# Seven products instead of eight in the attention's output projection, and a fixed order of transposes and products on TensorE

## The chip, the cores and the metric

The kernel runs on one core of one Trainium2 chip. A core has TensorE (PE in the profile; PEld are its weight loads), VectorE (DVE), ScalarE (ACT), GpSimd (POOL) and SyncE (SP), which here only issues DMAs. The metric is device time in microseconds (us) for one execution; lower is better.

## The reference

One layer of an encoder for two sequences of 1024 rows and 1024 columns. Attention and a Fourier mixing run side by side on the same normalised input and share one output projection; a feed-forward part (FFN) follows. What matters here is the attention and its half of the projection:

```python
def attend(args):
    qn_b, qp_b = args
    sc = (jnp.einsum('bqhd,bkhd->bhqk', qn_b, k_nope)
          + jnp.einsum('bqhr,bkr->bhqk', qp_b, k_pe)).astype(jnp.float32) * scale
    p = jax.nn.softmax(sc, axis=-1).astype(v.dtype)
    return jnp.einsum('bhqk,bkhd->bqhd', p, v)
...
mix = jnp.concatenate([y_mla, y_four], axis=-1) @ w_out
x = x + ga1 * mix
h2 = rmsnorm(x, g_ffn) * (1.0 + sc2) + sh2
ffn = (jax.nn.silu(h2 @ w_gate) * (h2 @ w_up)) @ w_down
return x + ga2 * ffn
```

The attention has 4 heads of width 128, so its half of the projection multiplies 512 columns by a 512 x 1024 part of `w_out`. Everything is float32. The kernel writes a product of two float32 matrices as three matmuls (`mm3`, lines 78 to 81): each operand is split into a high part (a cast on ScalarE, line 63) and a low part (the difference, line 64, on VectorE unless told otherwise), and high x high, high x low and low x high are added up.

## The kernel before

**Stages.** Up to about 282 us of the profile: adaLN, input projection and Fourier mixing. Then the attention of both sequences, to about 714 us; then the FFN, by products of half matrices, to the end. The attention is what the change touches, with its turn into the FFN.

**The attention** is a loop of 64 items k, one for each sequence s, block b of 256 rows, head h and half block u of 128 rows. Eight items make a block; r is k mod 8. Step k does, in the program's order:

- `scores(k)`: ten matmuls of 512 columns into `ps_s`; VectorE takes the maximum (`mx`, `nb`), ScalarE the exponential into `p`, VectorE scales by the reciprocal of the sum.
- in r = 3 and 4 `rope_q` (six matmuls of 256 columns and the rotary arithmetic, with `hv`, for the next block), in r = 5 and 6 `rope_flip` (four transposes into `pqt`, read out into `qp`), and in odd steps `absorb_q` (six matmuls of 256 columns, split into `qa`).
- `values` in r = 5 and 1: 24 matmuls of 512 columns for two heads and 256 rows, split into the high and low parts `o0b` and `o1b`.
- `flip_p(k-1)`: eight transposes of the probabilities of the item before, in two groups (`ppt`), each split into `pt`.
- ten steps behind its first score, the projection of a block: `out_proj` in r = 2, 4, 6 and 0, one for each u and each half g of the 1024 columns. Each is 12 matmuls (four heads, three each) into a bank `gb`, added on VectorE to the row tile `x`, which already holds the residual and the Fourier part. `norm2` normalises a finished row tile (ScalarE's square, six small GpSimd operations, VectorE's scaling into `xn`) in r = 4 and 0, `flip_h` transposes it (eight transposes, `pht`) in r = 6 and, for the other half, in r = 2.

The weights of the projection are made twice, for each sequence: loaded (`wv_load`), multiplied on GpSimd by the gate row `gah` (`wv_gate`, in steps 5 and 9 and in 37 and 41; the row's second half is loaded between) and split into `wv` (`wv_split`, eight splits in steps 6 to 11 and 39 to 43).

**The order.** The program is written with tiles; a scheduler puts each engine's instructions in a fixed order ahead of time, by the program's order and by when it expects the operands. `tc.issue_after(i)` holds the instructions under it behind instruction i, `first(early, late)` puts one before another, and `behind()` means behind the last split. Where neither stands, the scheduler may put transposes in the middle of a product. A tile with `bufs=n` has n buffers, and a writer waits for the reader of the oldest. `gb` and the transposes' banks have two each.

**The turn into the FFN.** Blocks (0,0) to (1,1) are projected in the loop. Block (1,2) is projected in steps 64 to 67, around the last `flip_p` and the last `values`; its row tiles are loaded in steps 60 and 61. Block (1,3) follows in four products behind the loop. Between them stand the FFN's preparations: `prep_h` splits the transposed rows into `H` (halves of 128 x 1024), `sums_w` makes four sums of the first FFN weights, `flip2` transposes the rows of block (1,2) and `norm3` normalises those of (1,3). `tail.close()` gives the memory back.

## Time and profile before

| | us |
|---|---|
| median of three runs | 1994.22 (1994.19 to 1996.29) |
| the profiled execution | 1991.72 |
| its span, first to last instruction | 1989.9 |
| attention, from the profile's timeline | about 282 to 714 |
| granted TensorE clock, mean | 0.998 |

The profile is one execution. In a timeline a row gives start, duration, engine, line, operation, output <- inputs, shapes and how many were merged; in brackets stands the idle time before it and what ended it. Matmuls are pipelined, and the durations shown overlap: what a matmul costs TensorE is the distance between two starts. A group row gives busy time and mean duration in ns, then the engine's idle time just before.

### The profile page before, as it was taken

How to read it: one execution, taken by the hardware profiler on the slowest of the kernel's cores; microseconds unless marked ns; L12 is line 12 of the kernel's file. 1: busy time of each engine (PE TensorE's matmuls, PEld its weight loads, DVE VectorE, ACT ScalarE, POOL GpSimd, SP SyncE). 2: the span in 40 equal slices, each digit the busy share in tenths (PEclk: the TensorE clock that was granted, in tenths of full speed). 3: DMA queues.
4: the chain of work that ended last, by engine and by line, in shares of the span. 5: the costliest groups of instructions: out<-in, count | busy, mean ns of one | idle time of the engine just before them, and what ended most of it. 6: DMA issues, size and time to landing. Idle time of an engine off the chain costs nothing.

```text
span 1989.9 us, 27639 instructions
## 1 busy us (share of the span) xinstructions
PE 1965.3 (99%) x9554; PEld 1621.7 (81%) x9554; DVE 1382.5 (69%) x2081; ACT 893.7 (45%) x1743; POOL 831.0 (42%) x1008
## 2 busy tenths in 40 slices
PE   8999999999999999999999999999999999999998
PEld 6788778888888878888888888888888888888886
DVE  5667767666777687877767668779655665656794
ACT  5764545555565563333333355443333333335551
POOL 2554012111312348977877401345644544510152
PEclk9999999999999999999999999999999999999999
DMA  9986965535354584654655597774322322357762
GB/s 392 333 318 227 358 237 116 110 91 160 101 117 138 191 283 166 218 181 172 200 182 190 171 316 231 239 230 150 133 96 90 132 94 92 116 199 241 254 228 85
DMA packets 167081, 377.12 MB, mean 190 GB/s; under 512 B 18044, under 2 KB 43260, under 8 KB 163740
## 3 DMA queue, kind: packets, MB, share of 16 engines
q1 hardware_dynamic: 144252, 304.03, 45.2%
q0 software_dynamic: 22112, 70.27, 11.4%
...
## 4 chain that ended last, share of the span: by engine, by line
PE 59%; DVE 2%; issue 1%; POOL 1%; DMA 1%; ACT 0%; SPq 0%; POOLq 0%; DVEq 0%; ACTq 0%
PE bank L80 20%; PE bank L79 20%; PE bank L81 20%; DVE wl L64 1%; DMA draw<-in_w_down_dram 1%; DVE val L1987 0%; DVE val L154 0%; DVE val L1878 0%; DVE H L64 0%; DMA val<-x_d 0%; POOL rs_y L107 0%; POOL val L154 0%; DVE val L151 0%; POOL out_dram L1993 0%; DVE val L1875 0%
## 5 line engine op out<-in xcount | busy, mean ns | idle before, releaser
L79 PE MATMUL bank<-H,wh 128*128 128x512 f32 x1232 | 480.2, 390 | 2.6 <-DVE val L154 0.9
L80 PE MATMUL bank<-H,wh 128*128 128x512 f32 x1232 | 479.5, 389 | 0.3 <-DVE H L64 0.3
L81 PE MATMUL bank<-H,wl 128*128 128x512 f32 x1232 | 479.3, 389 | 0.2 <-DVE wl L64 0.2
L79 PEld LDWEIGHTS bank<-H,wh 128*128 128x128 f32 x1232 | 231.2, 188 | 53.2 <-DVE val L1861 2.0
L64 DVE TENSOR_TENSOR wl<-draw,wh 128x512 fp32r<-128x512 f32 x286 | 209.0, 768 | 94.0 <-ACT wh L63 93.5
L81 PEld LDWEIGHTS bank<-H,wl 128*128 128x128 f32 x1232 | 231.3, 188 | 49.0 <-DVE wl L64 0.5
L80 PEld LDWEIGHTS bank<-H,wh 128*128 128x128 f32 x1232 | 231.3, 188 | 48.2 <-DVE H L64 0.6
L154 DVE TENSOR_TENSOR val<-bank,val 128x512 f32<-128x512 f32 x200 | 136.6, 689 | 163.0 <-PE bank L81 162.1
L63 ACT CAST wh<-draw 128x512 fp32r<-128x512 f32 x286 | 164.9, 619 | 173.2 <-PE bank L80 131.6
L154 POOL TENSOR_TENSOR val<-val 128x512 f32<-128x512 f32 x58 | 82.4, 1421 | 345.7 <-DVE val L1959 163.5
L80 PE MATMUL bank<-wl,wh 128*128 128x512 f32 x572 | 223.2, 390 | 0.8 <-DVE wl L64 0.5
L63 ACT CAST wh<-rgu 128x512 fp32r<-128x512 f32 x172 | 107.1, 623 | 258.4 <-PE bank L80 203.2
L81 PE MATMUL bank<-wh,wl 128*128 128x512 f32 x572 | 222.6, 389 | 0.0
L79 PE MATMUL bank<-wh 128*128 128x512 f32 x572 | 222.6, 389 | 0.0
L63 ACT CAST wh<-val 128x512 fp32r<-128x512 f32 x133 | 82.3, 622 | 261.9 <-PE bank L80 249.3
L64 DVE TENSOR_TENSOR wl<-val,wh 128x512 fp32r<-128x512 f32 x133 | 126.1, 950 | 65.4 <-ACT wh L63 65.3
L64 DVE TENSOR_TENSOR wl<-rgu,wh 128x512 fp32r<-128x512 f32 x172 | 162.5, 945 | 0.8 <-ACT wh L63 0.7
L151 POOL TENSOR_TENSOR val<-rgu 128x512 f32<-128x512 f32 x80 | 108.3, 1354 | 78.7 <-DMA rgu<-in_wgu_dram 74.9
L80 PEld LDWEIGHTS bank<-wl,wh 128*128 128x128 f32 x572 | 107.4, 188 | 25.2 <-DVE wl L64 2.9
L79 PEld LDWEIGHTS bank<-wh 128*128 128x128 f32 x572 | 107.4, 188 | 22.5
L81 PEld LDWEIGHTS bank<-wh,wl 128*128 128x128 f32 x572 | 107.4, 188 | 21.9
L151 POOL TENSOR_TENSOR val<-val 128x512 f32<-128x512 f32 x89 | 119.1, 1356 | 1.3
...
## 6 DMA issues: line engine op xcount, KB each, us to landing
...
```

The source lines that it names most:

```text
L63: here["a"] = nc.scalar.copy(hi, src).ins
L64: here["v"] = (eng or nc.vector).tensor_tensor(out=lo, in0=src, in1=rd(hi), op=ALU.subtract).ins
L79: nc.tensor.matmul(out, lh, rh, start=first, stop=False, skip_group_check=cont)
L80: nc.tensor.matmul(out, lh, rl, start=False, stop=False, skip_group_check=cont)
L81: here["t"] = here["pe"] = nc.tensor.matmul(out, ll, rh, start=False, stop=last, skip_group_check=cont).ins
L151: return eng.tensor_tensor(out=out, in0=x, in1=y, op=ALU.subtract).ins
L154: eng.tensor_tensor(out=out, in0=x, in1=y, op=ALU.add)
```

## The change

The projection of a block is a product of two matrices that are each cut in 2 x 2: the rows of the block by u and the heads by pairs (a11, a12, a21, a22), the weights by pairs of heads and by g (b11, b12, b21, b22). Winograd's form of Strassen's method needs seven products of such parts instead of eight, with sums around them:

- weights: b12 - b11, b22 - b12, b22 - (b12 - b11) and b21 - that, made in place by `wv_sum` on GpSimd; seven parts are split, fourteen splits a sequence;
- rows: `left_half` (at the first `values` of a block) makes a11's split and s3 = a11 - a21; `right_half` (at the second) splits a12 and a22 and makes s2, a21 + a22 and s4; the low parts of the sums are made on GpSimd (`low`);
- products m1 to m7, six matmuls each, one a step in r = 2 to 7 and 0, in the order of `PROD`; m1 is copied to `u`, m6 is added to it, and that goes to three quarters of the rows on GpSimd; the others are added on VectorE to one or two quarters each.

Every product is held behind the step's `flip_p`, and `flip_h` behind the product. `norm2` and `flip_h` take u = 1 first. `rope_flip` goes from r = 6 to 7. `p`, `qp`, `qa` and `hv` lose one buffer each, `H60` and `H61` are allocated when the tail is closed, and the rows of (1,3) are normalised in place. Block (1,2) has four of its products in steps 58 to 61 and three behind `flip_p(62)`; its row tiles are loaded in step 57.

```diff
     def half(name):
-        return e.tile([P, 512], F32, tag="hv", name=name, bufs=2)
+        return e.tile([P, 512], F32, tag="hv", name=name, bufs=1)
...
-        qp = e.tile([P, HEADS, P], F32R, tag="qp", name="qp", bufs=4)
+        qp = e.tile([P, HEADS, P], F32R, tag="qp", name="qp", bufs=3)
...
-        qa = [e.tile([P, 256], F32R, tag=f"qa{i}", name=f"qa{i}", bufs=3) for i in range(2)]
+        qa = [e.tile([P, 256], F32R, tag=f"qa{i}", name=f"qa{i}", bufs=2) for i in range(2)]
...
+    PROD = ("m1", "m7", "m6", "m5", "m4", "m2", "m3")
+    WEIGHT = {"m1": 0, "m2": 1, "m3": 2, "m5": 3, "m6": 4, "m7": 5, "m4": 6}
...
+    def low(t, src, eng):
+        here["a"] = nc.scalar.copy(t[0], src).ins
+        eng.tensor_tensor(out=t[1], in0=src, in1=rd(t[0]), op=ALU.subtract)
+
+    def left_half(s, b, po):
+        f = S["f", s, b] = {"a21": rest("fa"), "s3": rest("fs")}
+        o = S["o", s, b] = {"m1": part("oa")}
+        nc.scalar.copy(f["a21"], po[:, :, 1, :])
+        split(*o["m1"], po[:, :, 0, :])
+        sub(f["s3"], po[:, :, 0, :], f["a21"], nc.vector)
+
+    def right_half(s, b, po):
+        f, o = S["f", s, b], S["o", s, b]
+        for k, u in (("m2", 0), ("m4", 1)):
+            o[k] = part(("ob", "oc")[u])
+            split(*o[k], po[:, :, u, :])
+        s2, s4 = rest("ft"), rest("fu")
+        sub(s2, po[:, :, 1, :], f["s3"], nc.vector)
+        add(f["a21"], f["a21"], po[:, :, 1, :], nc.vector)
+        sub(s4, po[:, :, 0, :], s2, nc.vector)
+        for k, v in (("m6", s2), ("m5", f["a21"]), ("m3", s4)):
+            o[k] = part(f"o{k}")
+            low(o[k], v, nc.gpsimd)
...
-        for h in range(HEADS):
-            mm3(pm, o[0][:, h, us], o[1][:, h, us], wv[0][:, h, gs], wv[1][:, h, gs], h == 0, h == HEADS - 1)
-        here["v"] = nc.vector.tensor_tensor(out=x2[:, gs], in0=x2[:, gs], in1=pm, op=ALU.add).ins
+        for c in range(2):
+            with tc.issue_after(here["tp"]):
+                mm3(pm, lh[:, c, :], ll[:, c, :], wv[0][:, wi, c, :], wv[1][:, wi, c, :], c == 0, c == 1)
+        if k == "m1":
+            S["u"] = tl.tile([P, 512], F32, tag="u", name="u", bufs=1)
+            nc.scalar.copy(S["u"], pm)
+            o["m7"] = part("oa")
+            low(o["m7"], S.pop(("f", s, b))["s3"], nc.gpsimd)
...
+        for u, g in {"m1": ((0, 0),), "m7": ((1, 0), (1, 1)), "m5": ((1, 1), (0, 1)), "m4": ((1, 0),), "m2": ((0, 0),),
+                     "m3": ((0, 1),)}.get(k, ()):
+            to(u, g, pm)
+        if k == "m6":
+            here["v"] = nc.vector.tensor_tensor(out=S["u"], in0=S["u"], in1=pm, op=ALU.add).ins
+            for u, g in ((1, 0), (1, 1), (0, 1)):
+                to(u, g, S["u"], nc.gpsimd)
...
-                nc.tensor.transpose(pt[:, c, :], xn[:, (4 * g + c) * P : (4 * g + c + 1) * P], ident)
+                with tc.issue_after(here["t"]):
+                    nc.tensor.transpose(pt[:, c, :], xn[:, (4 * g + c) * P : (4 * g + c + 1) * P], ident)
...
-        if i % 2 == 0:
-            out_proj(s, b, i // 4, i // 2 % 2)
-        if i in (2, 6):
-            norm2(s, b, i // 4, tl)
-        if i == 4:
-            flip_h(s, b, 0)
+        if i < 7:
+            out_proj(s, b, i)
+        if i in (4, 6):
+            norm2(s, b, 3 - i // 2, tl)
+        if i == 6:
+            flip_h(s, b, 1)
...
-            p = w.tile([P, N], F32, tag="p", name="p", bufs=3)
+            p = w.tile([P, N], F32, tag="p", name="p", bufs=2)
...
+        def wv_sum(out, x, y):
+            for c in range(2):
+                o, x_, y_ = (S["wv", 2 * (blk // 2) + c, blk % 2] for blk in (out, x, y))
+                with tc.issue_after(here["p"]):
+                    here["p"] = sub(o, x_, y_, nc.gpsimd)
...
+        for q, k0 in enumerate((4, 36)):
+            for i in range(8):
+                todo[k0 + i // 4].append(lambda i=i: wv_gate(i))
+                if i == 3:
+                    todo[k0].append(lambda q=q: gate_half(q, 1))
+            for d, k, blk, sums in ((2, "m1", 0, ((0, 1, 0), (1, 3, 1))), (4, "m7", 1, ()), (4, "m3", 3, ((3, 3, 0),)),
+                                    (5, "m6", 3, ()), (6, "m5", 0, ()), (6, "m2", 2, ((2, 2, 3),)), (7, "m4", 2, ())):
...
-            todo[60 + u].append(lambda u=u: out_load(1, 2, u))
+            todo[57].append(lambda u=u: out_load(1, 2, u))
...
+                if k == nit:
+                    out_proj(1, 2, 4)
+                    norm2(1, 2, 1, tl)
+                    for i in (5, 6):
+                        out_proj(1, 2, i)
+                    S["tail", 3] = here["v"]
...
-                    if i in (5, 6):
-                        rope_flip(*nxt[:2], i - 5, tbank)
+                    if i in (5, 7):
+                        rope_flip(*nxt[:2], i // 2 - 2, tbank)
...
+            if 48 <= m < 52:
+                out_proj(1, 2, m - 48)
...
-        for n in range(4):
-            out_proj(1, 3, n // 2, n % 2)
-            if n == 1:
-                norm3(0)()
-            prep_step((2, 0, 0, 0)[n])
-            if n == 1:
+        for n in range(7):
+            out_proj(1, 3, n)
+            if n == 4:
+                norm3(1)()
+            prep_step((0, 2, 0, 0, 0, 0, 0)[n])
+            if n == 4:
```

81 lines of the change are left out of this document (36 added, 45 removed).

## The prediction

> **What bounds the kernel now.** I read the page's busy table first, then the busy time by stretches, then TensorE's own timeline, because its busy figure counts pipelined matmuls twice.
>
> ```profile
> PE 1965.3 (99%) x9554; PEld 1621.7 (81%) x9554; DVE 1382.5 (69%) x2081; ACT 893.7 (45%) x1743; POOL 831.0 (42%) x1008
> ```
> ```profile
> 440.00:494.60 54.60, 54.46 (x301) 46.10 (x300) 36.01 (x69) 30.13 (x63) 8.41 (x20) 1.00 0.57 141
> 714.00:722.00 8.00, 6.85 (x29) 4.76 (x27) 7.86 (x13) 7.25 (x12) 1.63 (x2) 1.00 0.87 297
> 722.00:730.00 8.00, 7.67 (x35) 6.25 (x36) 8.00 (x8) 7.59 (x9) 6.52 (x8) 1.00 0.56 204
> 730.00:738.00 8.00, 7.34 (x39) 5.86 (x38) 7.93 (x12) 4.34 (x9) 1.86 (x2) 1.00 0.79 277
> 738.00:746.00 8.00, 8.00 (x37) 6.62 (x36) 7.97 (x9) 5.34 (x11) 5.09 (x4) 1.00 0.66 215
> 746.00:754.00 8.00, 8.00 (x37) 6.53 (x36) 5.57 (x7) 2.37 (x4) 7.59 (x8) 1.00 0.53 188
> ```
>
> The columns of the stretches are length, then busy time of PE, PEld, DVE, ACT and POOL, the granted clock, the DMA share and GB/s. The first is one block of the attention (eight steps): TensorE is full, VectorE has 36.0 us of 54.6. The others are the start of the FFN: there VectorE is full from 714 to 746 (31.8 of 32 us) and TensorE has gaps. So a matmul saved inside the attention is time saved; one saved just ahead of 714 is not, unless VectorE also gets there earlier.
>
> ```profile
> 403.32 0.40 PE L79 MATMUL gb<-pt,ckv 128*128 128x512 f32 x1
> ...
> 408.54 0.39 PE L81 MATMUL gb<-pt,ckv 128*128 128x512 f32 x1
> 408.77 1.03 PE L1424 MATMUL ppt<-ident,p 128*128 128x128 f32 x8
> 409.56 0.48 PE L1395 MATMUL ps_s<-lat,qa 128*128 128x512 f32 x1
> 409.88 0.40 PE L1396 MATMUL ps_s<-lat,qa 128*128 128x512 f32 x1
> ...
> 412.22 0.63 PE L1424 MATMUL ppt<-ident,p 128*128 128x128 f32 x4
> 412.60 0.47 PE L79 MATMUL gb<-wv,o0b 128*128 128x512 f32 x1
> 413.06 0.66 PE L1424 MATMUL ppt<-ident,p 128*128 128x128 f32 x4
> 413.47 0.48 PE L80 MATMUL gb<-wv,o0b 128*128 128x512 f32 x1
> 413.79 0.40 PE L81 MATMUL gb<-wv,o1b 128*128 128x512 f32 x1
> ```
>
> From the 1st to the 24th matmul of one `values` the starts move by 5.22 us: **0.227 us a matmul of 512 columns**, though each is shown as 0.39. Eight transposes in a row take 0.79 us, and the matmul behind them 0.32, which is 0.09 more. Split by one matmul (412.22 to 413.79) the same eight and two matmuls take 1.57 us, against 0.79 + 0.32 + 0.23 = 1.34 together.
>
> **The change, part by part.**
>
> *Products.* Before, a block takes 4 products of 12 matmuls, after 7 of 6: 42 for 48. Over eight blocks 48 fewer, 48 x 0.227 = **-10.9 us**, if TensorE is the limit wherever they go.
>
> ```profile
> 423.36 0.39 PE L80 MATMUL gb<-wv,o0b 128*128 128x512 f32 x1
> 423.88 0.96 PE L1424 MATMUL ppt<-ident,p 128*128 128x128 f32 x7
> ```
>
> *Order.* Counted in the timeline, a block has 13 runs of transposes; after the change 12. At most 0.23 (the split above), 0.09 (a run) and 0.29 are won, the last in step r = 0, where two matmuls of a product go ahead of `flip_p` and the transposes start 0.52 us after the second instead of 0.23. Against that, nothing fills in for late probabilities. Bounds over six blocks 0 and -3.6; I take **-2.0**.
>
> *Work of the other engines in a block.*
>
> ```profile
> L1404 DVE TENSOR_REDUCE mx<-ps_s 128x1 f32<-128x1024 f32 x9 | 11.0, 1222 | 7.8 <-PE ps_s L1399 7.8
> L64 DVE TENSOR_TENSOR pt<-ppt,pt 128x512 fp32r<-128x512 f32 x16 | 10.5, 682 | 0.4 <-ACT pt L63 0.3
> L1411 DVE TENSOR_SCALAR p<-p,rr 128x1024 f32<-128x1024 f32 x8 | 6.1, 760 | 0.2
> L1343 DVE TENSOR_TENSOR x<-x,gb 128x512 f32<-128x512 f32 x4 | 2.7, 678 | 0.5 <-PE gb L81 0.5
> L64 DVE TENSOR_TENSOR qa<-gb,qa 128x256 fp32r<-128x256 f32 x4 | 1.7, 416 | 0.0
> L64 DVE TENSOR_TENSOR o1b<-gb,o0b 128x512 fp32r<-128x512 f32 x2 | 1.4, 693 | 5.7 <-ACT o0b L63 5.7
> L1409 ACT ACTIVATE p<-ps_s,nb 128x1024 f32<-128x1024 f32 x8 | 9.0, 1120 | 1.8 <-DVE nb L1405 1.7
> L63 ACT CAST qa<-gb 128x256 fp32r<-128x256 f32 x4 | 1.5, 372 | 4.2 <-PE gb L81 4.2
> L1468 POOL TENSOR_TENSOR wvr<-wvr,gah x16: 1277/1290/1748, 295.4 to 545.4; 128x512 f32<-128x512 f32 x16
> ```
>
> VectorE loses 4 adds and 2 splits (4 x 0.678 + 2 x 0.693 = 4.1 us) and gets 9 adds of 512 columns and 7 operations of 256 (3 low parts, 3 differences, 1 sum; the form of `qa`): 9 x 0.678 + 7 x 0.416 = 9.0. Net +4.9: 40.9 us in a block of about 52.9. ScalarE gets eight casts of 0.372 and one copy twice as wide for two casts twice as wide, +2.2. GpSimd gets 3 adds of 1.29 and 4 differences half as wide: +6.5 on 8.4. None becomes the bound on average. In step r = 3 it is close: 3.7 us of softmax and `pt`, 1.4 of the rotary query, 0.4 of `qa`, 1.4 for the two adds of m7 make 6.8 us, times 0.9 because neighbours overlap (the forms of that block sum to 40.2 where 36.0 are busy) 6.1 us, beside TensorE's ten scores, twelve half-wide matmuls, eight transposes and six matmuls, 5.9 us. What queues there drains in r = 5, where `values` alone gives 5.4 us. Between the last score of a step and the transposes of its probabilities stand at least eight transposes, six matmuls and the next ten scores, with the half-wide ones 5.2 us.
>
> *Weights.* Fourteen splits a sequence for eight, and eight GpSimd differences, in steps 4 to 11 and 36 to 43. The second four gatings follow the first in the next step, not four later, behind the load of the gate's other half, which itself waits for the first four. GpSimd stands there, with the norm chains of steps 38 and 40 behind it; the transposes of those rows come two steps later, which covers it. In steps 38 to 43 TensorE has some 36 us; VectorE has 0.77 x 36 = 27.9 and 14 x 0.68 = 9.5, or 37.4: 1.3 us too much there. Bounds: 0 if hidden, 12 x 0.68 = 8.2 if all the new ones are in the open; near the lower end, **+1.5**.
>
> *The last block's turn.* Four products of block (1,2) go up to steps 58 to 61 and three stay, behind `flip_p(62)`.
>
> ```profile
> 682.00 0.39 PE L1399 MATMUL ps_s<-lat,qp 128*128 128x512 f32 x1
> 683.62 0.74 DVE L1411 TENSOR_SCALAR p<-p,rr 128x1024 f32<-128x1024 f32 x1
> 694.94 0.39 PE L81 MATMUL gb<-pt,ckv 128*128 128x512 f32 x1
> 707.10 0.98 PE L1647 MATMUL pht<-ident,xn 128*128 128x128 f32 x7 [0.78 <-DVE xn L1353]
> 714.55 0.39 PE L79 MATMUL bank<-H,wh 128*128 128x512 f32 x1
> ```
> ```profile
> L64 DVE TENSOR_TENSOR H<-H,H 128x1024 fp32r<-128x1024 f32 x6 | 7.1, 1219 | 0.0
> ```
>
> The last score starts at 682.00, so TensorE is free at 682.23. The probabilities of item 62 are scaled at 684.36; before, a product stood in that gap. After, the products there must follow the transposes: 684.36 - 682.23 = 2.1 us, or 0.9 if VectorE scales before it takes the maximum of item 63 (1.2 us, in between). I take the upper end, **+2.1**, since that order is not touched.
>
> Then `values` ends: its last matmul starts at 694.94, the FFN's first at 714.55, 19.4 us after that matmul's 0.23. In them lie 72 matmuls of products; after the change 36 (one product of (1,3), m1, can stand before `values`). So 8.2 of the 10.9 us are to be had here. VectorE, though, has from there on: 5 operations of the right half (2.1), the 4 sums of the first FFN weights (2.7), 9 adds (6.1), 4 halves of `H` (4.9), two norms like the scaling of `p` (1.5): 17.3 us, times 0.9 some 15.6, and starts 0.3 after `values`. Its adds also give back the two `gb` banks, so TensorE waits with it. The FFN then starts about 16.0 us after `values`: 3.4 earlier instead of 8.2, **+4.8** lost. Bounds: +1 if VectorE is no limit (one wait like that of 0.78 us at 707.10 remains), +8.2 if the start doesn't move at all, since VectorE is full from 714 on.
>
> *At nothing.* `p` with 2 buffers: the exponential of item k needs the transposes of k-2, which TensorE ends a step before; uncovered it costs one exponential, 1.1 us, a step. `qp` 3, `qa` 2, `hv` 1: the last reader of the buffer is a step or a head earlier; uncovered, a cast of 0.4. `rope_flip` in step 7 has `absorb_q` behind it, so the transposes' banks come back in time. The row loads of (1,2) go from steps 60 and 61 to 57 in SP's queue, ahead of later `comb_h` loads; their buffers come free with the norms of (1,1) in 54 and 56. `H60` and `H61` behind the tail's end: split only after the FFN's first weights. `norm3` in place waits on its own store, which the norm's chain covers; if not, VectorE's adds queue behind it, within the turn's bound of 8.2.
>
> *Sum.* -10.9 - 2.0 + 1.5 + 2.1 + 4.8 = **-4.5 us**. The profiled execution took 1991.72 us (span 1989.9 and 1.8 around it), so 1987.2. It lies 2.5 us under the median of the runs; against the median 1994.22 that is **1989.7 us**.
>
> **The rivals.**
>
> A. *VectorE is no limit at the turn:* TensorE's order there can be filled and the 36 matmuls are saved whole. For it: in the attention VectorE idles a third. Against: 31.8 of 32 us behind it. -10.9 - 3 + 0.5 + 1 + 1 = -11.4, or 1982.8.
>
> B. *The FFN doesn't start earlier:* VectorE's extra adds eat the turn. For it: the full stretches. -10.9 - 1 + 1.5 + 2.1 + 8.2 = -0.1, or 1994.1.
>
> C. *Softmax becomes the limit of the steps (slower).* The place is the 5.2 us between a step's scores and its transposes. The chain there has maximum 1.22, exponential 1.12, scaling 0.76 and small ones, some 4.0 with the time between them (an estimate: 3.1 in the rows), plus whatever stands ahead on VectorE. It decides from 1.2 us of queue on, that is when two adds stand ahead in r = 3, 4, 6. GpSimd also slows VectorE:
>
> ```profile
> 641.48 0.75 DVE L1411 TENSOR_SCALAR p<-p,rr 128x1024 f32<-128x1024 f32 x1
> 651.67 1.58 DVE L1411 TENSOR_SCALAR p<-p,rr 128x1024 f32<-128x1024 f32 x1
> ```
> ```profile
> 650.97 1.74 POOL L151 TENSOR_TENSOR hcb<-hca 128x512 f32<-128x512 f32 x1
> ```
>
> The same scaling takes 0.75 us alone and 1.58 while GpSimd subtracts, and GpSimd gets 6.5 us more a block. With 0.6 us in three steps of six blocks, 10.8 us, the sum is +6.3, or 2000.5. [...]
>
> D. *TensorE's clock falls in the gap at the turn.* If the wait of the turn, 4.8 us, lies in one piece and the granted clock halves for as long afterwards, 4.8 us give half the matmuls: +2.4, so -2.1 in all, or 1992.1.
>
> ```profile
> 0.00:10.00 10.00, 4.76 (x20) 4.50 (x21) 3.52 (x14) 1.50 (x2) 1.69 (x9) 1.00 0.84 309
> ```
>
> Here TensorE idles 5.2 us of 10 and the clock is given as 1.00, which speaks against it. [...]
>
> That the change doesn't do what it says: the product count is fixed by the program, but the order already is nearly the new one (13 runs for 12); that is the 0 in the order's bounds.
>
> **How the numbers follow.** Forecast 0.45 (its own range -1.5 to -8), A 0.25, B 0.14, C 0.12, D 0.04. A measurement of this kernel can tell about 0.2%, 4 us, from no change. Faster by more: A and 0.27 of the forecast's 0.45 (its middle is only just past 4 us), 0.52. Within: the other 0.18, B and D, 0.36. Slower: C, 0.12. The range from 1983 to 1997 leaves out the far half of A and most of C; it takes in the weights' bound of 8.2 us.
>
> **What would show it.** Right: a block of 52.9 us in the attention; 336 matmuls that read `wv` instead of 384; a wait of some 2 us on `p` behind item 63's scores; VectorE full from the end of `values`, the FFN's first matmul some 16 us behind it, with TensorE waiting on adds (`gb`) or on `wl`. Wrong: a block above 53.5 with waits on `nb` or `p` in steps 3, 4 and 6 (C); FFN's start 12 us or less behind `values` (A) or still 19 (B); waits in steps 38 to 43 on `wv` above 2 us.

## The result, and the profile after

The changed kernel takes 2024.03 us (median of four runs, 2022.76 to 2025.32); the kernel before, on the same chip, 1994.2 us (1991.45 to 1996.29). The ratio is 1.015, 95% interval 1.0133 to 1.0168: **slower by some 30 us**, where 1989.7 was forecast and 1997 was the end of the range. The profiled execution after took 2022.76 us, with a span of 2020.6.

The page of the changed kernel, its busy table and the line of the granted clock (40 slices of the span, tenths):

```profile
PE 1966.4 (97%) x9506; PEld 1617.6 (80%) x9506; DVE 1435.0 (71%) x2173; ACT 917.3 (45%) x1811; POOL 911.6 (45%) x1080
PEclk9999999999999989999999999999999999999999
```

TensorE has 48 matmuls fewer (9506 for 9554), as it should, and a busy time that is no shorter. The span is 30.7 us longer, so TensorE now has time in which it has nothing to do, or works slowly: one slice has a granted clock of only 8 tenths.

Where the time went is read from TensorE's own timeline. `values` starts sixteen times, at marked places of the attention, and the FFN's first matmul reads `wh`. These rows of the changed kernel (start, duration, engine, line, operation) are the starts of `values` groups 1, 3, 9, 12, 15 and 16, the last matmul of group 16, and the FFN's first:

```profile
301.16 0.40 PE L79 MATMUL gb<-pt,ckv 128*128 128x512 f32 x1
...
355.45 0.48 PE L79 MATMUL gb<-pt,ckv 128*128 128x512 f32 x1
...
515.20 0.48 PE L79 MATMUL gb<-pt,ckv 128*128 128x512 f32 x1
...
607.01 0.40 PE L79 MATMUL gb<-pt,ckv 128*128 128x512 f32 x1
...
686.01 0.40 PE L79 MATMUL gb<-pt,ckv 128*128 128x512 f32 x1
...
707.28 0.48 PE L79 MATMUL gb<-pt,ckv 128*128 128x512 f32 x1
...
713.02 0.39 PE L81 MATMUL gb<-pt,ckv 128*128 128x512 f32 x1
...
742.45 0.50 PE L79 MATMUL bank<-H,wh 128*128 128x512 f32 x1 [0.71 <-ACT wh L63]
```

The same starts in both kernels give this table. The last columns are the product matmuls counted in the stretch (those that read `wv`), what their difference is worth at 0.227 us each, and what is left over.

| stretch (groups) | before, us | after, us | difference | products before, after | worth | left |
|---|---|---|---|---|---|---|
| to group 1 | 300.7 | 301.2 | +0.5 | 0, 0 | 0 | +0.5 |
| first preparation of weights (1 to 3) | 48.0 | 54.3 | +6.3 | 24, 18 | -1.4 | **+7.7** |
| three undisturbed blocks (3 to 9) | 163.9 | 159.8 | -4.1 | 144, 126 | -4.1 | 0.0 |
| second preparation (9 to 12) | 81.4 | 91.8 | +10.4 | 72, 66 | -1.4 | **+11.8** |
| late steps (12 to 15) | 76.5 | 79.0 | +2.5 | 48, 60 | +2.7 | -0.2 |
| last scores (15 to 16) | 19.2 | 21.3 | +2.1 | 24, 24 | 0 | +2.1 |
| turn (16 to the FFN) | 24.85 | 35.2 | +10.3 | 72, 42 | -6.8 | **+17.1** |
| the rest | 1275.4 | 1278.1 | +2.7 | | | +2.7 |

The last row is no effect of the change in itself: over all kernels below that keep the FFN's order, the rest lies between 1275.4 and 1279. In the experiments "turn" is from group 15 to the FFN: 44.1 us before, 56.4 after.

**The saving is there where nothing disturbs it.** A window of one block in the changed kernel (columns as in the prediction: length; PE, PEld, DVE, ACT, POOL; granted clock; DMA share; GB/s):

```profile
408.80:462.06 53.26, 53.26 (x295) 44.79 (x294) 40.17 (x79) 31.99 (x70) 14.45 (x28) 1.00 0.43 100
```

TensorE is full and VectorE has 40.2 us, close to the 40.9 that were worked out.

**What is lost lies in two places.** The waits of TensorE in the changed kernel (who waited for what: us in total, times, longest), the largest ones of the attention and the turn:

```profile
PE gb L79 <- DVE xn L1386: 6.8, 2, 5.8
...
PE ppt L1476 <- DVE nb L1457: 4.6, 4, 2.1
PE ppt L1476 <- DVE p L1463: 3.1, 3, 2.1
PE gb L79 <- DVE fu L151: 2.9, 1, 2.9
PE ps_s L1449 <- DVE qa L64: 2.8, 2, 2.0
...
PE gb L79 <- DVE qt L1022: 2.1, 1, 2.1
...
PE pht L1705 <- DVE xn L1404: 2.0, 1, 2.0
```

`p`, `qa` and `qt` belong to the preparations; the longest wait on `nb` is that of the last scores, the 2.1 us forecast there (VectorE makes `nb` of item 63 right behind the scaling of p(62), and the wait is put down to it); `xn` at line 1386, `fu` and `xn` at line 1404 are the turn. All that are shown are waits for VectorE. In the stretches of the two preparations TensorE's waits come to 6.4 and 7.6 us (1.5 of these for ScalarE), where the kernel before has 0.6 and none.

*Preparation.* A stretch of the second one in the changed kernel, first VectorE's and GpSimd's timelines, then TensorE's (in brackets: idle before, and what ended it):

```profile
527.61 3.01 POOL L1517 TENSOR_TENSOR wvr<-wvr,gah 128x512 f32<-128x512 f32 x2 [3.47 <-DMA gah<-ga_d]
...
529.46 1.71 DVE L64 TENSOR_TENSOR wv<-wvr,wv 128x512 fp32r<-128x512 f32 x1
531.09 1.75 DVE L1463 TENSOR_SCALAR p<-p,rr 128x1024 f32<-128x1024 f32 x1
...
536.05 1.75 DVE L1404 TENSOR_SCALAR xn<-x,rs_r 128x1024 f32<-128x1024 f32 x1 [2.08 <-POOL rs_r L111]
```
```profile
532.98 1.39 PE L1476 MATMUL ppt<-ident,p 128*128 128x128 f32 x8 [2.05 <-DVE p L1463]
...
534.60 0.63 PE L80 MATMUL gb<-wv,ob 128*128 128x512 f32 x1
535.02 0.63 PE L81 MATMUL gb<-wv,ob 128*128 128x512 f32 x1
```

GpSimd waits 3.5 us for its load and then multiplies just while VectorE splits weights. The split takes 1.71 instead of 0.68, the scaling of `p` behind it 1.75 instead of 0.75, and the transposes wait 2.05 us. VectorE itself then stands for 2.08 us before the norm's scaling, whose reciprocal root comes from GpSimd behind the gatings. Behind TensorE's wait the eight transposes take 1.39 us (1.03 elsewhere) and matmuls start 0.42 apart, not 0.23: TensorE runs at half speed for a while (granted clock 0.58 in 532.98:536.73).

*Turn.* The whole stretch before, then after, and four microseconds of it:

```profile
689.70:714.55 24.85, 24.03 (x113) 19.43 (x112) 16.31 (x21) 13.51 (x22) 7.78 (x21) 1.00 0.76 274
```
```profile
707.30:742.50 35.20, 22.30 (x86) 16.42 (x83) 20.95 (x30) 15.95 (x28) 14.80 (x26) 0.85 0.61 218
...
724.00:728.00 4.00, 4.00 (x10) 3.09 (x10) 2.12 (x4) 3.26 (x5) 2.42 (x5) 0.50 0.85 333
```

Before, TensorE was busy in 24.0 of 24.9 us there. After, no engine is: VectorE has 21 of 35 us, GpSimd nearly twice what it had. That looks like a chain of waits, not like a full engine. TensorE's four longest waits there, and the GpSimd row behind the last of them:

```profile
716.27 0.47 PE L79 MATMUL gb<-wv,oa 128*128 128x512 f32 x1 [2.87 <-DVE fu L151]
...
723.65 0.77 PE L79 MATMUL gb<-wv,oa 128*128 128x512 f32 x1 [5.77 <-DVE xn L1386]
...
730.71 0.87 PE L1705 MATMUL pht<-ident,xn 128*128 128x128 f32 x6 [1.99 <-DVE xn L1404]
...
738.72 0.50 PE L79 MATMUL gb<-wv,ob 128*128 128x512 f32 x1 [1.06 <-DVE xn L1386]
```
```profile
734.20 3.75 POOL L1386 TENSOR_TENSOR xn<-xn,u 128x512 f32<-128x512 f32 x3 [4.33 <-DVE u L1392]
```

Read in order: m1 of (1,3) waits until `fu`, the last operation of the right half, has read the bank of `values`; m7 waits for m1's add, which stands on VectorE behind two halves of `H` and three of the four sums; the transposes wait for the norm behind (1,2)'s last add, itself held behind the fourth sum; m2 waits for an add that VectorE makes only when GpSimd has done m6's three adds. The releasers show this sequence; which link is worth what, only the runs can show. The waits of 6.8, 2.9, 2.0 and 0.7 us on TensorE and one of 0.4 make 12.8, where before there was one of 0.8; 14 matmuls of the stretch start 0.43 apart, 2.9 us more; together 14.9 of the 17.1 left over.

### The profile page after: what moved, and what is told of

Its sections match the earlier page's. It is cut to its first block, busy times and chain, and to the rows that moved or that the text cites. A ratio compares the mean times of both kernels' runs of the same rounds, so it can differ in the third digit from the quotient of the medians.

```text
span 2020.6 us, 27899 instructions
## 1 busy us (share of the span) xinstructions
PE 1966.4 (97%) x9506; PEld 1617.6 (80%) x9506; DVE 1435.0 (71%) x2173; ACT 917.3 (45%) x1811; POOL 911.6 (45%) x1080
## 3 DMA queue, kind: packets, MB, share of 16 engines
q10 hardware_dynamic: 576, 1.05, 0.1%
## 4 chain that ended last, share of the span: by engine, by line
PE 84%; DVE 6%; DMA 3%; POOL 3%; ACT 2%; issue 2%; SPq 0%; POOLq 0%; ACTq 0%; DVEq 0%
PE bank L79 22%; PE bank L80 22%; PE bank L81 22%; PE gb L79 2%; PE gb L80 2%; PE gb L81 2%; PE ppt L1476 2%; PE ps_s L1449 1%; PE ps_s L1450 1%; PE ps_s L1451 1%; PE ps_s L1447 1%; PE ps_s L1448 1%; DVE mx L1456 1%; DVE wv L64 1%; DVE p L1463 1%
```

## The experiments

All results in one table: time of the kernel (the median with the 95% interval of its ratio to the kernel before, or a single run) and the stretches, read as above.

| kernel | time, us | ratio to before | first prep. | 3 blocks | second prep. | late | turn | rest |
|---|---|---|---|---|---|---|---|---|
| before | 1994.2 | 1 | 48.0 | 163.9 | 81.4 | 76.5 | 44.1 | 1275.4 |
| after | 2024.03 | 1.0133 to 1.0168 | 54.3 | 159.8 | 91.8 | 79.0 | 56.4 | 1278.1 |
| b_order | 1997.9 | single run | 47.9 | 163.9 | 81.4 | 76.5 | 46.2 | 1278.9 |
| a_free | 2019.0 | single run | 54.3 | 158.9 | 88.7 | 77.8 | 57.4 | 1277.7 |
| a_nosum | 2014.6 | single run | 51.2 | 159.7 | 87.2 | 79.0 | 56.6 | 1278.1 |
| a_sumdve | 2027.6 | single run | 57.5 | 159.7 | 93.1 | 78.9 | 57.6 | 1277.9 |
| a_spread | 2020.2 | single run | 51.5 | 161.8 | 89.4 | 79.0 | 56.4 | 1278.5 |
| a_eight | 2020.7 | 1.0114 to 1.0145 | 50.0 | 160.3 | 90.3 | 79.0 | 57.9 | 1277.3 |
| a_none | 2011.0 | 1.0067 to 1.0097 | 48.1 | 160.3 | 85.0 | 79.0 | 56.4 | 1278.3 |
| n_gate | 2009.7 | 1.0056 to 1.0086 | 48.1 | 160.2 | 82.4 | 79.0 | 58.0 | 1277.2 |
| a_turn | 2025.2 | single run | 54.3 | 159.5 | 91.6 | 79.0 | 54.4 | 1283.2 |
| a_banks | 2023.0 | single run | 54.3 | 159.7 | 91.5 | 79.0 | 57.9 | 1276.8 |
| a_both | 2020.6 | single run | 51.5 | 161.8 | 90.3 | 78.9 | 56.3 | 1278.1 |
| a_cover | 2027.7 | 1.0147 to 1.0178 | 54.6 | 159.7 | 92.8 | 78.9 | 61.3 | 1276.8 |
| a_norm | 2023.4 | 1.0128 to 1.0162 | 54.4 | 159.7 | 92.9 | 79.0 | 56.2 | 1276.3 |
| a_early | 2027.0 | 1.014 to 1.0174 | 54.3 | 159.6 | 91.6 | 79.0 | 54.9 | 1284.5 |
| a_fill | 2026.0 | 1.0138 to 1.0169 | 54.3 | 159.6 | 91.5 | 79.0 | 58.9 | 1277.4 |
| a_first | 2022.1 | 1.012 to 1.015 | 54.3 | 159.7 | 91.8 | 79.0 | 54.1 | 1277.2 |
| a_fb | 2021.4 | 1.0123 to 1.0157 | 54.3 | 159.7 | 92.7 | 79.0 | 53.8 | 1276.9 |
| a_best | 2030.4 | 1.0156 to 1.0187 | 56.6 | 161.8 | 90.3 | 79.2 | 55.6 | 1285.5 |

Each stretch is from one profiled execution. How far it repeats is seen in kernels whose edit does not touch it: the late steps are 78.9 to 79.2 wherever the products' order stands, the first preparation 54.3 to 54.6, the second 91.5 to 92.9, the turn 56.4 to 58.0. So 1 us can be read in the first two of these, but only some 2 us in the second preparation and at the turn. The turn column holds the last scores too, and in some kernels these take 22.9 us instead of 21.3, since the clock is halved there (see the last section). Where that matters, the time from group 16 to the FFN is given: 35.2 us in the changed kernel, 34.8 to 36.7 in the seven kernels in which the turn is as the change made it.

### The order of transposes and products

**b_order**: the kernel before, with the order alone.

```diff
-            mm3(pm, o[0][:, h, us], o[1][:, h, us], wv[0][:, h, gs], wv[1][:, h, gs], h == 0, h == HEADS - 1)
+            with tc.issue_after(here["tp"]):
+                mm3(pm, o[0][:, h, us], o[1][:, h, us], wv[0][:, h, gs], wv[1][:, h, gs], h == 0, h == HEADS - 1)
...
-                nc.tensor.transpose(pt[:, c, :], xn[:, (4 * g + c) * P : (4 * g + c + 1) * P], ident)
+                with tc.issue_after(here["t"]):
+                    nc.tensor.transpose(pt[:, c, :], xn[:, (4 * g + c) * P : (4 * g + c + 1) * P], ident)
```

> The kernel before, with only the new order: each product held behind the step's flip_p, flip_h behind the product; eight products as before. Theory 1 (the order is nearly the old one and harmless): within 3 us of the kernel before, a steady block of the attention 54.0 to 54.8 us for 54.6. Rival (the order is what costs, since no product fills in for late probabilities): 10 us or more slower, a block of 56 or more.

The blocks take 163.9 us with it and without; only the last scores change, where the turn column grows from 44.1 to 46.2. So the order is worth nothing in the blocks, and costs the 2.1 us at p(62). The time is 2.9 us above the 1995.0 of the kernel before, run beside it: theory 1.

**a_free**: the changed kernel without the order (the same two holds taken out).

```diff
-            with tc.issue_after(here["tp"]):
+            with ExitStack():
                 mm3(pm, lh[:, c, :], ll[:, c, :], wv[0][:, wi, c, :], wv[1][:, wi, c, :], c == 0, c == 1)
...
-                with tc.issue_after(here["t"]):
+                with ExitStack():
```

> The changed kernel without the fixed order: products and flip_h free again. Theory 1 (the cost lies in the weights' preparation and in the turn to the FFN, not in the order): still 2012 us or more, 0 to 10 us less than the changed kernel, the turn (from the last values to the FFN's first matmul) still above 30 us for 35.2. Rival (the order costs): 1998 or less.

The blocks gain 0.9 us, the late steps 1.2 and the second preparation 3.1: where probabilities are late, a product may now go ahead of their transposes. The first preparation and the turn are as long as with the order, as theory 1 had it. So the order makes the second preparation's loss larger and is not the cause of it.

### The preparation of the weights

**a_nosum**: the changed kernel without the differences and sums of the weights on GpSimd, which are left out.

```diff
-                for out, x, y in sums:
+                for out, x, y in ():
```

> The changed kernel without the weights' sums (wv_sum left out: 8 GpSimd differences a sequence less; all splits stay, so the sums of the projection are not the reference's). Theory 1 (GpSimd's work beside VectorE's makes VectorE's instructions long and late): the stretch of the second preparation (fifth values of sequence 1's weights, 91.8 us from the 9th to the 12th values, for 81.3 before) comes to 86 or less, total 5 to 9 us less than the changed kernel. Rival (the number of splits on VectorE): 2 us less or no change.

The first preparation falls by 3.1 us, the second by 4.6. The second stands at 87.2 us, between theory 1's 86 and the rival's 89.8. GpSimd's eight operations a sequence are a part of the loss, though GpSimd itself is busy for no more than 27.3 of the first preparation's 54.3 us and 46.4 of the second's 91.8 in the changed kernel.

**a_sumdve**: the sums on VectorE instead.

```diff
-                    here["p"] = sub(o, x_, y_, nc.gpsimd)
+                    sub(o, x_, y_, nc.vector)
```

> The changed kernel with the weights' sums on VectorE instead of GpSimd: 8 x 0.7 = 5.6 us more for VectorE a sequence, 8 x 1.3 to 1.7 less for GpSimd. [...] Rival (VectorE's volume): 93 us or more.

3.2 and 1.3 us longer: the rival's 93 us. If GpSimd's interference (1.71 us for a split of 0.68, above) had been the whole price of the sums, the second preparation would have been shorter than 91.8 us. VectorE's own volume counts, and in the first preparation more; the 1.3 is within what the second varies by.

**a_spread**: the splits spread over eight steps instead of six.

```diff
-            for d, k, blk, sums in ((2, "m1", 0, ((0, 1, 0), (1, 3, 1))), (4, "m7", 1, ()), (4, "m3", 3, ((3, 3, 0),)),
-                                    (5, "m6", 3, ()), (6, "m5", 0, ()), (6, "m2", 2, ((2, 2, 3),)), (7, "m4", 2, ())):
+            for d, k, blk, sums in ((2, "m1", 0, ((0, 1, 0), (1, 3, 1))), (4, "m7", 1, ()), (5, "m3", 3, ((3, 3, 0),)),
+                                    (6, "m6", 3, ()), (7, "m5", 0, ()), (8, "m2", 2, ((2, 2, 3),)), (9, "m4", 2, ())):
```

> The changed kernel with the weights' splits at most two a step (m3 a step later, m6, m5 and m2 one, one and two, m4 two later), same number. Theory 1 (GpSimd beside VectorE is what counts, by a_nosum): the second preparation stays above 88 us of 91.8. Rival (too many splits in a step): 86 us or less, and the first 51 or less for 54.3.

The preparations lose 2.8 and 2.4 us, and the blocks behind the first one get 2.0 longer, where the last of the splits now stand. Theory 1's figure (89.4 us, above 88) came true. The single run is 3.9 us below the changed kernel's median, which is little more than single runs differ by.

**a_none**: four of seven weights split in each sequence, which is before's eight splits, and no sums; the products of m2, m4 and m5 read the prepared weights of m7, m6 and m1.

```diff
-    WEIGHT = {"m1": 0, "m2": 1, "m3": 2, "m5": 3, "m6": 4, "m7": 5, "m4": 6}
+    WEIGHT = {"m1": 0, "m2": 5, "m3": 2, "m5": 0, "m6": 4, "m7": 5, "m4": 4}
...
-                todo[k0 + d].append(lambda k=k, blk=blk: wv_split(k, blk))
+                if k in ("m1", "m7", "m3", "m6"):
+                    todo[k0 + d].append(lambda k=k, blk=blk: wv_split(k, blk))
...
-            for c in range(2):
+            for c in ():
                 o, x_, y_ = (S["wv", 2 * (blk // 2) + c, blk % 2] for blk in (out, x, y))
```

> The changed kernel that splits four of the seven prepared weights in each sequence (eight halves of 128x512, as many as before) and leaves out the weights' differences and sums; the products of m2, m4 and m5 read the prepared weights of m7, m6 and m1 in place of their own. Theory (VectorE's and GpSimd's volume in the preparation is the loss there): the first preparation stretch (54.3 us in the changed kernel, 48.0 before) falls to 47 to 49 us, the second (91.8, 81.4 before) to 79 to 82 us, which is before's less the products' saving; the turn stays at 56 to 57 us; the time falls by 15 to 19 us, to 2004 to 2008 us. Rival (the order of the products and of the softmax chain in those steps is the loss, the volume is covered): both stretches stay within 4 us of the 51.2 and 87.2 that leaving the sums out alone gave, and the time stays at 2012 to 2015 us.

The first preparation is at 48.1, before's figure: there the six further splits and the sums are nearly the whole loss. The second falls by 6.8 us to 85.0, not to the 79 to 82 expected, and the time by 13 instead of 15 to 19. The theory is right for the first; in the second something else stands there too.

**a_eight**: the same four splits, with all the sums made.

```diff
-    WEIGHT = {"m1": 0, "m2": 1, "m3": 2, "m5": 3, "m6": 4, "m7": 5, "m4": 6}
+    WEIGHT = {"m1": 0, "m2": 5, "m3": 2, "m5": 0, "m6": 4, "m7": 5, "m4": 4}
...
+                if k in ("m1", "m7", "m3", "m6"):
```

> The changed kernel that splits four of the seven prepared weights in each sequence, with all the differences and sums still made on GpSimd; the products of m2, m4 and m5 read other prepared weights. Theory (volume; the two parts add up): the stretches lie above those of the kernel without splits and sums by what the sums alone were worth, 3.1 and 4.6 us: 50 to 52 us and 83 to 86 us, and the time is 2011 to 2016 us. Rival (the sums hurt only because the six further halves stand beside them): the stretches are within 1.5 us of those of the kernel with neither.

Without the further splits the first preparation falls by 4.3 us, to the 50.0 expected, without the sums by 3.1, without both by 6.2: roughly additive. The second falls by 1.5, 4.6 and 6.8, and the 83 to 86 us expected are missed, as is the time (2020.7 for 2011 to 2016). Of these only the last two are clear of what this stretch varies by; what the further splits cost there by themselves isn't shown.

**n_gate**: a_none, with the second four gatings of the second sequence in step 39 instead of 37.

```diff
-                todo[k0 + i // 4].append(lambda i=i: wv_gate(i))
+                todo[k0 + i // 4 * (1, 3)[q]].append(lambda i=i: wv_gate(i))
```

> The kernel without the three further splits and the sums (it splits four weights in each sequence; the products of m2, m4 and m5 read other prepared weights), with the second four gatings of the second sequence in step 39 instead of 37, behind the norm of step 38. Theory (what is left there, 85.0 us where 79.4 were due, is the norm that the change moved to step 38: its reciprocal root waits on GpSimd behind gatings that wait 3.4 us for their load, and VectorE and the softmax behind it wait in turn, and TensorE runs the next matmuls at half its clock): the second preparation stretch falls from 85.0 to 79.5 to 82 us, the wait on rs_r goes, and the time falls by 3 to 5 us, to 2006 to 2008 us. Rival (the splits' subtractions beside GpSimd's gatings are enough): it stays at 84 to 86 us.

The second preparation falls from 85.0 to 82.4 us, 0.4 above the end of the range, and away from the rival's 84 to 86. The time falls by 1.3 us only, not by 3 to 5; the turn, which the edit does not touch, is 1.6 us longer in the profiled execution. VectorE's and GpSimd's timelines in n_gate, at the same place as above:

```profile
514.76 3.78 POOL L1517 TENSOR_TENSOR wvr<-wvr,gah 128x512 f32<-128x512 f32 x3
...
526.67 5.92 POOL L1517 TENSOR_TENSOR wvr<-wvr,gah 128x512 f32<-128x512 f32 x4
```
```profile
523.56 0.67 DVE L64 TENSOR_TENSOR wv<-wvr,wv 128x512 fp32r<-128x512 f32 x1
524.15 0.75 DVE L1463 TENSOR_SCALAR p<-p,rr 128x1024 f32<-128x1024 f32 x1
...
526.75 1.77 DVE L1404 TENSOR_SCALAR xn<-x,rs_r 128x1024 f32<-128x1024 f32 x1 [0.72 <-POOL rs_r L111]
```

With GpSimd idle, split and scaling take 0.67 and 0.75 us again, the norm of step 38 waits 0.7 us for its reciprocal root (2.08 in the changed kernel), and no matmul of the stretch runs at half speed (eleven in the changed kernel, six in a_none). Now it is the norm's own scaling that meets a gating, at 1.77. The change had put gatings, their load, the first splits and, by `norm2` for u = 1 first, a norm into the same few steps (36 to 38).

### The turn into the FFN

**a_turn**: without the hold that puts the weights' sums of the FFN ahead of the add of (1,2)'s last product.

```diff
-            first(here["s"], S["tail", 3])
```

> The changed kernel, with the add of block (1,2)'s last product no longer held behind the sums of the FFN's first weights. Theory 1 (at the turn the two gb banks wait behind VectorE's queue; one is held by that add): the turn comes to 29 us or less for 35.2, total about 6 us less. Rival (VectorE's volume at the turn is the limit): 33 us or more, total within 2 us.

The turn is 2.0 us shorter, 33.1 us from group 16, which is the rival's figure and not the theory's 29. The rest is 5.1 longer, longer than in any kernel that keeps this hold; what it pays is shown with a_early.

**a_banks**: four banks of their own for the products of (1,3).

```diff
-        pm = gbank()
+        pm = S.get("gbank", gbank)()
...
+        xb_ps = tail.enter_context(tc.tile_pool(name="p4x_ps", bufs=1, space=PSUM, reuse_waits="tile"))
+        S["gbank"] = lambda: xb_ps.tile([P, 512], F32, tag="gx", name="gx", bufs=4)
```

> The changed kernel, with four PSUM banks of their own for the seven products of block (1,3) (the scores' banks, free by then) instead of the two gb banks. Theory 1 (at the turn TensorE waits for the two gb banks, whose adds stand behind the FFN's preparation on VectorE): from the last values to the FFN's first matmul 26 us or less for 35.2, no halved clock there, total 8 to 11 us less. Rival (VectorE's volume at the turn): 33 us or more, since the adds and the H halves are the same.

57.9 us, as long as any of the unchanged turns, and 35.0 from group 16: the rival's 33 or more. The banks alone are not the limit, though TensorE's waits are on `gb`; with them gone it waits 4.1, 3.8 and 3.7 us elsewhere, for an add, for the norm ahead of the transposes, and for ScalarE's `wh`.

**a_both**: a_banks and a_spread together.

```diff
-        pm = gbank()
+        pm = S.get("gbank", gbank)()
...
+            for d, k, blk, sums in ((2, "m1", 0, ((0, 1, 0), (1, 3, 1))), (4, "m7", 1, ()), (5, "m3", 3, ((3, 3, 0),)),
+                                    (6, "m6", 3, ()), (7, "m5", 0, ()), (8, "m2", 2, ((2, 2, 3),)), (9, "m4", 2, ())):
```

> a_banks and a_spread together. If the two are independent, the sum of their gains in total, within 3 us. With theory 1 for the turn and its rival for the weights it would be near 2005 us; with neither near 2024.

2020.6 us, as a_spread alone: the banks add nothing to it.

**a_cover**: the last three products of (1,2), 18 matmuls, behind the last `values` group instead of ahead of it.

```diff
-                if k == nit:
+                if k == nit + 2:
                     out_proj(1, 2, 4)
```

> The changed kernel with the last three products of the last but one block (18 matmuls, 4.1 us at 0.227) issued behind the last values group instead of ahead of it. Theory (the turn is a chain of waits through ScalarE, VectorE and GpSimd that has too little product work beside it): from the second last values group to the FFN 56.4 us falls by 3 to 6 us, to 50 to 53.5 us, with TensorE's waits on fu and on the add to xn (2.9 and 5.8 us) shortened by 4 us in sum and fewer half-speed matmuls there; the time falls to 2016 to 2021 us. Rival (the chain through the add, the norm and its transposes sets the end, and it begins with these products): they come later, so it ends later, and the turn is 57 to 61 us.

61.3 us, 0.3 above the rival's range. The two waits that the theory named did shrink, from 8.6 to 4.3 us in sum. But where the products had stood TensorE now waits 0.9 us more and runs at half speed, so that the last scores take 20.1 us where 17.2 were due without the 18 matmuls; and the transposes of (1,2) start 7.7 us later, with group 16 at the same time in both kernels, since the adds and the norm ahead of them come later. The rival was right: products moved to cover one wait uncover another and make the chain begin later.

**a_norm**: m6's three adds of (1,3) on VectorE.

```diff
-                to(u, g, S["u"], nc.gpsimd)
+                to(u, g, S["u"], None if (s, b) == (1, 3) else nc.gpsimd)
```

> The changed kernel with m6's three adds of the last block on VectorE instead of GpSimd, which then has only the norms' small steps there. Theory (the norm's chain on GpSimd, held up by those adds, is a link of the turn): xn is ready 2 to 4 us earlier and the turn falls from 56.4 to 53 to 55 us. Rival (VectorE's own work sets the turn): three adds more of 0.68 us each make it 56.4 to 58.5 us.

56.2 us: in the column neither the gain nor the loss shows. But the last scores of this execution ran into the half clock and took 22.9 us; from group 16 it is 33.3 us, 1.4 below the shortest unchanged turn, and TensorE's wait of 1.06 us ahead of m2 is gone. So the adds look like a link worth 1 to 2 us, which one execution cannot prove. In a_first (below), where other links are shorter, the same wait is 2.89 us:

```profile
730.04 3.74 POOL L1387 TENSOR_TENSOR xn<-xn,u 128x512 f32<-128x512 f32 x3 [5.54 <-DVE u L1393]
```
```profile
734.56 0.80 PE L79 MATMUL gb<-wv,ob 128*128 128x512 f32 x1 [2.89 <-DVE xn L1387]
```

The two edits together were not run.

**a_early**: the three products of (1,2) in steps 62 and 63, with a_turn's edit, which it needs.

```diff
-                if k == nit:
-                    out_proj(1, 2, 4)
-                    norm2(1, 2, 1, tl)
-                    for i in (5, 6):
-                        out_proj(1, 2, i)
-                    S["tail", 3] = here["v"]
+                pass
...
-            if 48 <= m < 52:
-                out_proj(1, 2, m - 48)
+            for i in {53: (5, 6)}.get(m, (m - 48,) if 48 <= m < 53 else ()):
+                out_proj(1, 2, i)
+                if i == 4:
+                    norm2(1, 2, 1, tl)
+                S["tail", 3] = here["v"]
...
-            first(here["s"], S["tail", 3])
```

> The changed kernel with the last three products of the last but one block in steps 62 and 63 instead of 64, and the sums not put ahead of the add of the last of them. Theory (the turn is set by the chain from this add through the norm to its transposes, as moving these products behind the values group made it 4.9 us longer): the chain begins 4 to 8 us earlier; from the second last values group to the FFN the 56.4 us fall to 46 to 52 us with 4.1 us of product work gone from there into the stretch before it (79.0 becomes 79 to 83), and start to FFN is 4 to 8 us less; the time is 2015 to 2020 us. Rival (VectorE's sums and H preparation set it wherever these products stand): the two stretches together stay at 134 to 137 us.

The turn is 54.9 us, no better than a_turn alone (54.4), and the rest 6.4 longer; the two stretches of the expectation are 133.9 us together, next to the rival's 134 to 137. The products do come 2.4 to 5.5 us earlier, counted from group 15, but the transposes of (1,2) start 35.7 us behind group 15 in a_early as in a_turn (44.7 in the changed kernel). What brings them forward is the lifted hold, and moving these products earlier adds nothing. Two rows of a_early, of VectorE and of TensorE, show what the rest pays:

```profile
744.98 0.75 DVE L1696 TENSOR_SCALAR xn<-xn,rs_r 128x1024 f32<-128x1024 f32 x1 [3.21 <-DMA x_d<-xn]
```
```profile
752.20 0.80 PE L80 MATMUL bank<-H,wh 128*128 128x512 f32 x1 [4.19 <-DVE H L64]
```

`norm3`, which the change does in place, has to wait for its own store, and VectorE stands 3.2 us with the splits of `H` behind it in its order (2.8 us in a_turn, none in the changed kernel). The FFN's second group of matmuls then waits 4.2 us for a part of `H`, where it waits 0.9 in the changed kernel. So these two edits gain at the turn and lose it again behind a wait that the prediction had put at nothing, rightly for the changed kernel. This is read from the rows; a kernel with the hold lifted whose `norm3` doesn't wait was not run.

**a_fill**: m4's product of (1,3) made four times over.

```diff
-        for c in range(2):
+        for c in (0, 1) * (4 if (s, b, k) == (1, 3, "m4") else 1):
```

> The changed kernel that makes m4's product of the last block four times over (18 matmuls more, 4.1 us at 0.227), ahead of the transposes that wait 5.8 us for the add to xn. Theory (the half clock behind the waits is a loss of its own, and a busy TensorE does not have it): the wait of 5.8 us falls to 1 to 2.5 us, the matmuls behind it run at 0.227 us each and not at 0.43, and although TensorE does 4.1 us more, the turn falls by 1 to 3 us, to 53.5 to 55.5 us. Rival (TensorE only waits for the chain, and the clock costs nothing since the chain is late anyway): 56 to 57.5 us. Second rival (no cover): 60 us.

58.9 us, above the first range and the first rival's, short of the second rival's 60. The place was badly chosen: the wait of 5.8 us stands ahead of m7, not of the transposes, so it stayed, and so did its half-speed matmuls. What the run does show: 18 more matmuls, 4.1 us, cost 2.5 in the turn, and the seven half-speed matmuls that the changed kernel has some 10 us into the FFN are not there. The price of the half clock by itself was not separated from that of the waits.

**a_first**: an order put back that the change had taken out. Before, five lines put the split of the FFN's first `H` ahead of the last values' split, of a norm's square and scaling, and of an add of block (1,2):

```diff
-            first(here["a"], S.pop(("tail", 5)))
-            first(here["v"], S.pop(("tail", 6)))
-            first(here["v"], S.pop(("tail", 2)))
-            first(here["v"], S["tail", 4])
-            first(here["a"], S.pop(("tail", 7)))
```

a_first adds to the changed kernel:

```diff
             split(*o[k], po[:, :, u, :])
+            S.setdefault(("rh", s, b), (here["a"], here["v"]))
...
             next(prep)
             next(prep)
+            for x, y in zip((here["a"], here["v"]), S["rh", 1, 3]):
+                first(x, y)
```

> The changed kernel with the order between the FFN's first prepared weight and the last values group put back, which the change took out with five lines: both halves of the split of H ahead of the right half's first split, on ScalarE and on VectorE. Theory (VectorE's own order sets the turn: it is idle for 3.8 us while TensorE works on the last values group, as before it did these splits in 690.6 to 692.9 us, and then has splits, sums and adds in one row): the two splits, 1.64 and 1.24 us, stand beside the values group, the add to xn for which TensorE waits 5.8 us comes 2.5 to 3.5 us earlier, the turn falls from 56.4 to 52.5 to 54.5 us, the rest stays at 1276 to 1279, and the time falls by 2 to 4 us, to 2019.5 to 2022 us. Rival (the chain through the banks, the norm and the transposes is as long as the add's): the wait of 5.8 us shrinks and another grows, and the turn stays at 55.5 to 57 us.

54.1 us, with the rest unchanged: as expected (the time, 2022.1, is just past the end of its range), and 2.3 us below the shortest of the unchanged turns; from group 16 it is 32.8 us, 1.9 below the shortest. VectorE's timeline at this place in the three kernels, before, after and a_first:

```profile
690.56 2.35 DVE L64 TENSOR_TENSOR H<-H,H 128x1024 fp32r<-128x1024 f32 x2
695.98 0.69 DVE L64 TENSOR_TENSOR o1b<-gb,o0b 128x512 fp32r<-128x512 f32 x1 [3.07 <-ACT o0b L63]
```
```profile
713.85 0.42 DVE L64 TENSOR_TENSOR ob<-gb,ob 128x256 fp32r<-128x256 f32 x1 [3.76 <-ACT ob L63]
...
717.55 1.64 DVE L64 TENSOR_TENSOR H<-H,H 128x1024 fp32r<-128x1024 f32 x1 [1.42 <-ACT H L63]
719.62 1.24 DVE L64 TENSOR_TENSOR H<-H,H 128x1024 fp32r<-128x1024 f32 x1 [0.43 <-ACT H L63]
...
722.83 0.68 DVE L1386 TENSOR_TENSOR xn<-xn,gb 128x512 f32<-128x512 f32 x1
```
```profile
709.68 2.35 DVE L64 TENSOR_TENSOR H<-H,H 128x1024 fp32r<-128x1024 f32 x2
...
715.71 1.22 DVE L151 TENSOR_TENSOR H<-rgu 128x512 f32<-128x512 f32 x1
...
720.85 0.68 DVE L1387 TENSOR_TENSOR xn<-xn,gb 128x512 f32<-128x512 f32 x1
```

Before, the two splits of `H` lay beside the last values' matmuls. After, VectorE is idle for 3.8 us there, and the splits stand between the values' end and the add that gives TensorE its bank back. Put back, the add comes 2.0 us earlier (1.6 counted from the end of `values`), not 2.9: the four sums now meet GpSimd's low parts and take 1.1 to 1.2 us each instead of 0.7.

**a_fb**: a_first and a_banks together.

```diff
-        pm = gbank()
+        pm = S.get("gbank", gbank)()
...
+            for x, y in zip((here["a"], here["v"]), S["rh", 1, 3]):
+                first(x, y)
```

> The same order put back, and four banks of their own for the last block's products (alone they left the turn at 57.9 us). Theory (two chains of like length, through VectorE and through the banks, cover each other): the turn falls below that of the order alone by 1.5 to 3 us, to 50 to 53 us. Rival (the norm's steps on GpSimd behind the adds end the turn in either case): it stays within 1 us of the order alone, and the wait moves to the add or norm ahead of the transposes.

53.8 us, within 0.3 of a_first: the rival's figure. Banks don't count here either.

### All together

**a_best**: a_early, n_gate's step 39 for the gatings, and the spread splits with the first sums a step later.

```diff
+            for d, k, blk, sums in ((2, "m1", 0, ()), (3, None, 0, ((0, 1, 0), (1, 3, 1))), (5, "m7", 1, ()), (5, "m3", 3, ((3, 3, 0),)),
+                                    (6, "m6", 3, ()), (7, "m5", 0, ()), (8, "m2", 2, ((2, 2, 3),)), (9, "m4", 2, ())):
...
-                todo[k0 + i // 4].append(lambda i=i: wv_gate(i))
+                todo[k0 + i // 4 * (1, 3)[q]].append(lambda i=i: wv_gate(i))
...
+            for i in {53: (5, 6)}.get(m, (m - 48,) if 48 <= m < 53 else ()):
```

> The changed kernel with the early products of the last but one block, the second gatings of the second sequence behind the norm of step 38, and the splits spread over eight steps with the first sums a step later. If the three losses are apart from each other, the first preparation stretch is 51 to 53 us, the second 85 to 89, the stretches from there to the FFN 127 to 133, and the time 2006 to 2014 us. Rival (what is taken out of one step comes up in the next, as the spread alone gave back 2.0 us in the undisturbed blocks): 2015 to 2020 us.

2030.4 us, slower than the change itself and above both ranges. The first preparation became longer (56.6), the blocks 161.8 as with the spread, and the rest 1285.5, as in a_turn and a_early (VectorE waits 2.8 us for the store here too). None of these kernels is faster than the kernel before. a_first, a_norm and a lifted hold without the wait for the store were never put together.

## Why the prediction was wrong, point by point

- **Products, -10.9: right where TensorE is the limit.** The three undisturbed blocks fall by 4.1 us, which is 18 matmuls of 0.227; the late steps and the last scores follow the count within 0.2 as well, once the wait below is taken off. In the other stretches the saving is covered by the losses below.
- **Order, -2.0: not there.** b_order shows 0.0 in the blocks, the lower of the two bounds. In the changed kernel taking the order out even gains 0.9 us in the blocks (a_free). The 13 runs of transposes counted before could not be turned into time.
- **Wait for p(62), +2.1: right.** The stretch of the last scores is 2.1 us longer in the changed kernel, and the turn column by the same in b_order.
- **Weights' preparation, +1.5 with bounds 0 and 8.2: the first step that failed.** It measured 7.7 + 11.8 = 19.5 us. Two things in it were wrong. VectorE's rate there was taken from its average in a block and its durations from rows in which GpSimd was quiet; the sum, 1.3 us too much in one preparation, left no room for operations that take more than twice as long beside GpSimd (1.71 us for 0.68, 1.75 for 0.75). And the bound of 8.2 counted new splits alone, at 0.68 each. a_none puts 6.2 and 6.8 us down to the splits and sums together; n_gate puts 2.6 more, just clear of what the stretch varies by, down to gatings, their load and a norm in the same steps. I had seen that GpSimd stands there with the norm chains behind it, and took it as covered by the transposes two steps later. It is not: the norm's scaling stands in VectorE's queue until GpSimd's root has come, and the softmax stands behind it, as rival C said for another place. So TensorE never waited on `wv`, the sign that I had named, but on `p`, `qa` and `qt`, which VectorE makes behind the splits and the norm. 2.4 us of the second preparation (82.4 in n_gate against the 80.0 that 81.4 - 1.4 makes) and 1.5 of the first (48.1 in a_none against 46.6) stay unexplained.
- **Turn, +4.8 with bounds 1 and 8.2: the second step that failed.** The forecast took VectorE as full from the end of `values` and added up its work, 15.6 us, so that the FFN would start 16.0 us behind the last values matmul. It started 742.45 - 713.02 - 0.23 = 29.2 us behind it, with VectorE busy in 19.0 of them: its work was near the 17.3 that I had listed, but it was not full. In place of a full engine the trace shows a chain that goes through ScalarE, VectorE, GpSimd and TensorE in turn, with 42 product matmuls beside it for 72; m1, which I had put ahead of `values`, waited for the bank behind it. Even B, no gain at all, would have been 19.4, and A, 12 or less, is further off still. One link is shown by a run: the order that the change took out costs 2.3 us (a_first). The diff had these five lines, and my working gave them no term; it counted four halves of `H` behind `values`, and there were six. m6's adds on GpSimd look like a second link, of 1 to 2 us. Banks, and the place of (1,2)'s products when they come earlier, are shown to gain nothing. How the rest of the 17.1 us divides among the links, some 13 to 15 us, is not settled; the waits and the half-speed matmuls listed above show where they lie.
- **Rival C** had the mechanism, softmax late behind VectorE's queue and VectorE slowed by GpSimd, but in the wrong place: the undisturbed blocks have no such loss, the preparations do. Its two rows (0.75 and 1.58 us for the same scaling) belonged into the preparation's term, where GpSimd's work was known to stand.
- **Rival D** was held down by one row, a stretch early in the kernel with the clock at 1.00 and TensorE idle for half of it. The half clock did come, in the second preparation and at the turn: behind TensorE's waits of 2.05, 2.00, 5.77 and 1.99 us the granted clock was 0.58 in 532.98:536.73, 0.52 in 571.0:574.5, 0.50 in 723.65:728.1 and 0.63 in 730.7:733.9. Some 34 matmuls ran at half speed from the attention's start to some 20 us into the FFN, where before it was one at most: 34 x 0.2 = 6.8 us. It comes behind waits (the last seven of these matmuls 1.0 us behind one of 0.90), so it was a factor on errors already made rather than an error by itself. That it lasts as long as the wait was D's own estimate; measured are 4.45 us at 0.50 behind the wait of 5.77, and 3.5 at 0.52 behind that of 2.00.
